# Gates turned by block transposes on VectorE and partition-exchanging DMAs, in a two-layer attention and convolution encoder on one core

## The chip, the cores and the metric

One core of a Trainium2 chip. The metric is the device time of one execution in microseconds (us), the median over runs.

## The reference: what is computed

Two layers (DEPTH 2), a sequence of 512 rows, model width 2048, all fp32. Each layer normalises the rows, multiplies them by one wide input projection, and cuts the result into latents, convolution inputs, memory queries and a gate as wide as the three groups' outputs together:

```python
h = rmsnorm(x, pre_norm_g[l])
z = h @ w_in[l]
q_lat, kv_lat, k_pe, gb, gc, xin, q_mem, gate = split_cols(z)
...
a_out = mla_attention(q, k, v)                 # 8 heads, width 1024
c_out = short_gated_conv(gb, gc, xin, conv_w[l])   # width 512
m_out = memory_attention(q_mem..., mem_n, w_mk[l], w_mv[l])   # 4 heads, width 512
y = jnp.concatenate([a_out, c_out, m_out], axis=-1) * jax.nn.silu(gate)
o = y @ w_o[l]
x = x + rmsnorm(o, post_norm_g[l])
```

The heads' outputs are needed with the features on the partitions (the output projection contracts over them), while the input projection leaves the gate with the sequence's rows on the partitions. So the gate has to be transposed before it multiplies a head's output.

## The kernel before, in words

**Products.** Every fp32 product is made of three matmuls of fp32r parts on TensorE (PE): high by high, low by high, high by low (`mm3`, lines 271 to 273). The large projections are made by a scheme of seven products P1 to P7 over 2x2 blocks. The input projection of a layer is five groups of columns, `gs[0]` to `gs[4]`, each two slabs of 512 columns wide (the fourth 416). `gs[2]` makes the memory heads' gate `gm` and the memory queries `qm`; `gs[4]`, in the code `g4`, makes the attention heads' gates `ga0` and `ga1` in 28 steps. A product ends with a function `final(i, j, tt)` for each finished tile of 128 rows; for these two groups it did nothing (`skip`).

**Order of the work.** A program of steps is written out in Python. `put` adds steps in a row, `weave` adds extra steps among others, `add` adds one. Each step names the weights (units) that it reads. A weight is loaded by SP's queue (line 145) some units ahead of its use, cast to its high part by ScalarE (ACT, line 188, `wh`) and its low part by VectorE (DVE, line 189, `wl`) two units ahead. Some weights are sums, and their second term is added by an accumulating DMA from GpSimd's queue (line 145 too, POOL). A step may put small work into a deferring queue (`pr.defer`), which is emptied as later steps leave room, or until a condition holds (`pr.until`). PE, SP and POOL run in the order in which the program wrote their instructions; ACT and DVE are put in order by a scheduler.

**The gate.** The result of a group stands in slabs of 128 partitions x 2048 (19 buffers), four row tiles of 512 columns. `gate_turn` (line 897) makes one quarter of a gate slab: `turn4` (line 886) transposes four tiles of 128x128 on PE into one bank of PSUM (line 889), and ACT takes Silu of the bank into the slab `y` (line 900). A slab thus takes 16 transposes and four Silus, a layer has three slabs. The memory heads' (`gm`) is turned at the end of the input projection; those of `ga0` and `ga1` in `mixer` (line 1214): `ga0` between the two rope products, `ga1` behind the second.

**The start of the mixer.** `mixer` first makes the rotated part of the queries for four heads: two products (`qr`), whose sums with the rope tables are made on DVE (lines 1019 to 1029) and split into `qrh` on ACT and the rest `rm` on DVE (lines 276 and 277). Then come the four memory heads, among whose steps the first pair of attention heads is prepared (`qkv`: two products for Q, two for K, two for V). A head has four query blocks. Each block is a score product (`sc`), its row maximum on DVE (line 1134, `nm`), exp with the row sum on ACT (line 1137), a reciprocal on DVE (line 1139, `rec`), a scaling on ACT (line 1140), transposes of the probabilities on PE (line 1150, `ptp`), and their split into high on ACT and low on DVE (lines 276 and 277, `PT`). When a memory head's four blocks are there, PE multiplies them with the values (`o`), and DVE multiplies the result by the gate (line 1165, `y<-o,y`). In the memory heads the blocks are handled in a pipeline: transposes follow their score three blocks later, and the first head's `o` stands behind the ninth score.

## Time and profile before

| | before |
|---|---|
| time, median of 3 runs | 1473.28 us (1473.27 to 1473.75) |
| the profiled execution's span | 1471.1 us; no time beside the span is recorded for it |
| PE busy | 1459.6 us, 99% |
| DVE / ACT / POOL busy | 1087.0 / 863.3 / 269.5 us |
| granted TensorE clock | 0.9 or more of full speed in every slice |
| 16 DMA engines | 288.91 MB in 142655 packets |

The span is that of one profiled execution, from its first to its last instruction; the medians are taken over other runs and count what lies around the span. A row of a timeline gives start, duration, engine, line, operation, what it writes and reads, and in brackets how long the engine sat idle before it and what ended that. Names are the program's with buffer numbers left out.

### The profile page before, as it was taken

The numbers are of one execution on the slowest core, as the hardware profiler recorded it, in microseconds if no ns is written. First come the engines' busy times: TensorE is split into PE (matmuls) and PEld (weight loads), VectorE is DVE, ScalarE is ACT, GpSimd is POOL, SyncE is SP. The second block draws the span as 40 slices with busy tenths as digits, with TensorE's granted clock in tenths as the row PEclk, the third lists the DMA queues.
The fourth block names the chain that finished last, engine by engine and source line by source line (L and its number), as shares of the span: only waits on it lengthen the run. The fifth ranks groups of instructions, "written<-read, shape, count | busy, mean of one in ns | idle before, by whom it ended". The sixth has DMA issues, their size and how long they took to land.

```text
span 1471.1 us, 19497 instructions
## 1 busy us (share of the span) xinstructions
PE 1459.6 (99%) x7200; PEld 1247.5 (85%) x7200; DVE 1087.0 (74%) x1445; ACT 863.3 (59%) x1316; POOL 269.5 (18%) x276
## 2 busy tenths in 40 slices
PE   9999999999999999999999999999999999999997
PEld 8888888899888888888898888888988888888886
DVE  5899677957557778868789666776575577788687
ACT  7856343445459788654777434434364686786443
POOL 0032302032301010321210333030322000003111
PEclk9999999999999999999999999999999999999999
DMA  9999979697964292695987999696979554128945
GB/s 358 402 274 225 218 185 187 171 187 221 207 202 107 79 275 89 124 231 154 339 290 228 232 234 222 194 177 161 206 200 216 171 142 104 40 87 155 262 112 186
DMA packets 142655, 288.91 MB, mean 196 GB/s; under 512 B 9888, under 2 KB 32928, under 8 KB 138720
## 3 DMA queue, kind: packets, MB, share of 16 engines
q0 software_dynamic: 56576, 129.51, 43.9%
q1 hardware_dynamic: 85984, 158.16, 33.0%
q8 instruction: 56, 0.92, 0.2%
q14 instruction: 39, 0.32, 0.1%
HBM read 266.01 MB, written 21.63 MB: 196 GB/s over the span
## 4 chain that ended last, share of the span: by engine, by line
PE 96%; DMA 2%; DVE 1%; ACT 0%; SPq 0%; issue 0%; POOLq 0%; DVEq 0%; ACTq 0%
PE P L271 23%; PE P L272 23%; PE P L273 23%; PE ptp L1150 2%; PE tps L889 2%; PE o L272 1%; PE sc L271 1%; PE sc L272 1%; PE sc L273 1%; PE o L273 1%; PE o L271 1%; PE qps L271 1%; PE sc L1131 1%; PE qps L272 1%; PE qps L273 1%; PE sc L1132 1%
## 5 line engine op out<-in xcount | busy, mean ns | idle before, releaser
L188 ACT CAST wh<-wr 128x1024 fp32r<-128x1024 f32 (+2 forms) x436 | 445.4, 1024 | 458.0 <-PE P L273 363.4
L189 DVE TENSOR_TENSOR wl<-wr,wh 128x1024 fp32r<-128x1024 f32 (+2 forms) x436 | 516.0, 1186 | 261.3 <-ACT wh L188 258.0
L271 PE MATMUL P<-wh,S 128*128 128x512 f32 (+1 forms) x896 | 345.1, 385 | 0.0
L272 PE MATMUL P<-wl,S 128*128 128x512 f32 (+1 forms) x896 | 343.7, 384 | 0.0
L273 PE MATMUL P<-wh,S 128*128 128x512 f32 (+1 forms) x896 | 343.2, 383 | 0.0
L271 PE MATMUL P<-wh,A 128*128 128x512 f32 (+1 forms) x656 | 253.0, 386 | 0.0
L272 PE MATMUL P<-wl,A 128*128 128x512 f32 (+1 forms) x656 | 251.8, 384 | 0.5 <-DVE wl L189 0.5
L273 PE MATMUL P<-wh,A 128*128 128x512 f32 (+1 forms) x656 | 251.7, 384 | 0.0
L145 POOL DMA_DIRECT2D wr<-in_w_in_dram x132 | 158.3, 1200 | 439.6 <-DVE wl L189 324.4
L273 PEld LDWEIGHTS P<-wh,S 128*128 128x128 f32 x896 | 168.2, 188 | 30.5
L272 PEld LDWEIGHTS P<-wl,S 128*128 128x128 f32 x896 | 168.2, 188 | 29.5
L271 PEld LDWEIGHTS P<-wh,S 128*128 128x128 f32 x896 | 168.1, 188 | 29.5
L272 PEld LDWEIGHTS P<-wl,A 128*128 128x128 f32 x656 | 123.2, 188 | 22.9 <-DVE wl L189 1.3
L273 PEld LDWEIGHTS P<-wh,A 128*128 128x128 f32 x656 | 123.1, 188 | 22.4
L271 PEld LDWEIGHTS P<-wh,A 128*128 128x128 f32 x656 | 123.1, 188 | 21.7 <-ACT og L579 0.2
L145 POOL DMA_DIRECT2D wr<-in_w_o_dram x40 | 48.5, 1258 | 297.8 <-DVE wl L189 290.9
L1137 ACT ACTIVATE P<-sc,nm 128x512 f32<-128x512 f32 (+1 forms) x96 | 59.7, 623 | 26.0 <-DVE nm L1134 25.7
L1140 ACT ACTIVATE P<-P,rec 128x512 f32<-128x512 f32 (+1 forms) x96 | 62.0, 659 | 8.3 <-DVE rec L1139 8.0
L1134 DVE TENSOR_REDUCE nm<-sc 128x1 f32<-128x512 f32 (+1 forms) x96 | 56.9, 593 | 12.5 <-PE sc L1132 9.6
L1150 PE MATMUL ptp<-identr,P 128*128 128x128 f32 x320 | 46.1, 272 | 0.0
L177 DVE TENSOR_TENSOR wr<-wr,wr 128x1024 f32<-128x1024 f32 (+1 forms) x36 | 42.3, 1177 | 4.5 <-DMA wr<-in_w_in_dram 3.9
L1150 PEld LDWEIGHTS ptp<-identr,P 128*128 128x128 f32 x320 | 38.0, 140 | 6.1
(318 smaller groups left out, 2072.3 us busy)
## 6 DMA issues: line engine op xcount, KB each, us to landing
wr<-in_w_in_dram SPq DMA_DIRECT2D x128, 512.0 KB, 5.4
wr<-in_w_in_dram POOLq DMA_DIRECT2D x108, 512.0 KB, 7.3
wr<-in_w_o_dram SPq DMA_DIRECT2D x48, 512.0 KB, 6.6
wr<-in_w_o_dram POOLq DMA_DIRECT2D x40, 512.0 KB, 6.9
wr<-in_w_in_dram SPq DMA_DIRECT2D x32, 416.0 KB, 3.7
wr<-in_w_in_dram POOLq DMA_DIRECT2D x24, 416.0 KB, 6.0
wr<-in_w_mk_dram SPq DMA_DIRECT2D x15, 512.0 KB, 8.6
wr<-in_w_mv_dram SPq DMA_DIRECT2D x15, 512.0 KB, 10.2
```

Of the source, the lines that this page charges most:

```text
L145: engine.dma_start(dst, src, **kw)
L177: nc.vector.tensor_tensor(tiles[a], tiles[a], tiles[b], op=ALU.add)
L188: pin(nc.scalar.copy(hi[:, h], src[:, h]))
L189: pin(nc.vector.tensor_tensor(lo[:, h], src[:, h], hi[:, h].bitcast(F32), op=ALU.subtract))
L271: nc.tensor.matmul(ps, ah, bh, start=first, stop=False, **kw)
L272: nc.tensor.matmul(ps, ah, bl, start=False, stop=False, **kw)
L273: nc.tensor.matmul(ps, al, bh, start=False, stop=last, **kw)
L889: nc.tensor.transpose(ps[:, t * P:(t + 1) * P], view(t)[:, j * P:(j + 1) * P], G["ident"])
L1134: nc.vector.tensor_reduce(nmax, ps, axis=AX.X, op=ALU.max, negate=True)
L1137: nc.scalar.activation(pt, ps, AF.Exp, bias=nmax, accum_out=tot)
L1140: nc.scalar.activation(pt, pt, AF.Copy, scale=rec)
L1150: nc.tensor.transpose(ps[:, k * P:(k + 1) * P], pt[:, k * P:(k + 1) * P], G["ident"])
```

## The change

The gates' slabs are stored in another order of columns (`p (c t k)`, viewed as four row tiles of 4x128). When a product of `gs[2]` or `gs[4]` ends, `gated` applies Silu on ACT, in place, or for the last products of `ga0` directly from PSUM (which leaves out a copy), and defers one DVE instruction that transposes the 32x32 blocks of the tile in place (`blocks_turned`, line 920 of the changed file). When all four tiles of a slab are so turned, `exchange` (line 922) sends 16 DMAs on SP's queue, one for each pair of a group of 32 partitions as source and one as destination; each moves 32 partitions x 16 runs x 32 elements, that is 64 KB in pieces of 128 bytes. They write the slab `y` that `gate_turn` wrote before. Three slabs per layer make 96 DMAs in all, 24 block transposes, and 96 transposes fewer on PE. The exchange of `gm` stands in the program behind step 13 of `g4`, that of `ga1` behind the first product for Q, that of `ga0` behind the fourth block of the memory heads. Without gates to turn, `mixer` puts the two rope products and their sums one behind the other, and the first product for Q ahead of the first score.

```diff
@@ input projection
         def own(*names):
             def f():
                 for n in names:
-                    C[n] = slab(n).rearrange("p (t c) -> p t c", t=NT)
+                    C[n] = slab(n).rearrange("p (c t k) -> p t c k", c=4, t=NT)
             return f
...
+        def gated(*names):
+            def fin(i, j, tt, ps=None):
+                if names[j] is None:
+                    return
+                v = C[names[j]][:, 2 * i + tt]
+                nc.scalar.activation(v, v if ps is None else ps, AF.Silu)
+
+                def turn():
+                    blocks_turned(v)
+                    C[names[j], "turned"] = C.get((names[j], "turned"), 0) + 1
+                pr.defer(0.7, turn)
+            return fin
+
+        fin_m, fin_a = gated("gm", None), gated("ga0", "ga1")
...
-            group(L, (l, 2), 512, block((O_G + 1536, O_QM), 512), slot_of("gm", "qm"), STEADY, skip),
+            group(L, (l, 2), 512, block((O_G + 1536, O_QM), 512), slot_of("gm", "qm"), STEADY, fin_m),
...
-            group(L, (l, 4), 512, block((O_G, O_G + 512), 512), slot_of("ga0", "ga1"), STEADY, skip),
+            group(L, (l, 4), 512, block((O_G, O_G + 512), 512), slot_of("ga0", "ga1"), STEADY, fin_a, direct=direct_a),
...
-    def gate_turn(j, view, c):
+    def blocks_turned(v):
+
+        nc.vector.transpose(v, v)
+
+    def exchange(dst, src):
+
+
+        for p in range(4):
+            for b in range(4):
+                a = src[32 * p:32 * p + 32].rearrange("i t c k -> i (c t) k")[:, :, 32 * b:32 * b + 32]
+                y = dst[32 * b:32 * b + 32].rearrange("i c (t k) -> i (c t) k", k=P)[:, :, 32 * p:32 * p + 32]
+                nc.sync.dma_start(y, a)
+
+    def gate_rows(k, name, C):
         def f():
-            ps = turn4(view, c)
-            nc.scalar.activation(y_slab(j // 4)[:, j % 4, :], ps, AF.Silu)
+            pr.until(lambda: C.get((name, "turned")) == NT)
+            exchange(y_slab(k), C[name])
         return f
...
@@ mixer
-    def mixer(l, C, gates, pair2, tail):
+    def mixer(l, C, pair2, tail):
...
-        gs = [(g, []) for g in gates]
         (p0, rotate0, fetch0), (p1, rotate1, fetch1) = (q_rope_steps(l, g) for g in range(2))
-        put(p0[:1], gs[:4], p0[1:])
-        put(rotate0, gs[4:])
+        put(p0, rotate0)
         sts = [{} for _ in range(4)]
         qkv = qkv_steps(l, 0, sts[0])
         qkv[0] += (0.0, 1)
         qkv[2] += (0.0, 0)
+        put(qkv[:1])
+        add(gate_rows(1, "ga1", C))
...
-        between = {k: [s] for k, s in zip((0, 2, 5, 8, 10, 12), qkv)}
+        between = {k: [s] for k, s in zip((2, 5, 8, 10, 12), qkv[1:])}
+        between.setdefault(3, []).append((gate_rows(0, "ga0", C), []))
...
-        put(g4[8:16])
+        put(g4[8:13])
+        add(gate_rows(3, "gm", C))
+        put(g4[13:16])
...
-        more = [(f, []) for f in lat + [qm_turn(j, C) for j in range(4)] + [gate_turn(12 + j, gm, j) for j in range(4)]]
-        put(weave(g4[16:], more[:12], 2, 2))
-        put(more[12:])
-        gates = [gate_turn(j, lambda t, C=C, j=j: C["ga0" if j < 4 else "ga1"][:, t, :], j % 4) for j in range(8)]
+        more = [(f, []) for f in lat + [qm_turn(j, C) for j in range(4)]]
+        put(weave(g4[16:], more, 2, 2))
```

In `group`, the PSUM bank is viewed as 4x128 where the slot is; `turn4` and the convolution read the new views.

**How it moves instructions.** Lines from 1103 on are 34 higher in the changed file: its exp is L1171, its scaling L1174, its row maximum L1168. First ACT at the start of layer 0's memory heads, from the table load to the first casts of transposed probabilities (`PT`). Before (`P<-sc,nm` is an exp, `P<-P,rec` a scaling):

```order
L1137 ACT_TABLE_LOAD
L1137 ACTIVATE P_3811,tot_3812<-sc_3805,nm_3809 128x256
L276 CAST Q_3819<-qps_3820 128x512
L1140 ACTIVATE P_3811<-P_3811,rec_3814 128x256
L1137 ACTIVATE P_3841,tot_3842<-sc_3835,nm_3839 128x256
L1137 ACTIVATE P_3853,tot_3854<-sc_3847,nm_3851 128x256
L1140 ACTIVATE P_3841<-P_3841,rec_3844 128x256
L1140 ACTIVATE P_3853<-P_3853,rec_3856 128x256
L276 CAST Q_3819<-qps_3859 128x512
L276 CAST PT_3886<-ptp_3887 128x2x128
L1137 ACTIVATE P_3880,tot_3881<-sc_3874,nm_3878 128x256
L276 CAST PT_3886<-ptp_3904 128x2x128
```

The changed kernel, from the first exps to the first casts; the rows left out are three more exps, seven scalings and the second cast for Q:

```order
L1171 ACT_TABLE_LOAD
L1171 ACTIVATE P_3810,tot_3811<-sc_3804,nm_3808 128x256
L1171 ACTIVATE P_3822,tot_3823<-sc_3816,nm_3820 128x256
L1174 ACTIVATE P_3810<-P_3810,rec_3813 128x256
...
L1171 ACTIVATE P_3913,tot_3914<-sc_3907,nm_3911 128x256
L1171 ACTIVATE P_3943,tot_3944<-sc_3937,nm_3941 128x256
L1171 ACTIVATE P_3965,tot_3966<-sc_3959,nm_3963 128x256
...
L1171 ACTIVATE P_3983,tot_3984<-sc_3977,nm_3981 128x256
L1174 ACTIVATE P_3983<-P_3983,rec_3986 128x256
L276 CAST PT_3884<-ptp_3885 128x2x128
L276 CAST PT_3884<-ptp_3902 128x2x128
L276 CAST K_3922<-kps_3923 128x512
```

The first PT cast stood behind three exps and three scalings; it now stands behind nine of each.

Second, DVE at the same place, around the first row maximum (`nm`); `rm` is the rope sum, `wl` a weight's low part. Before:

```order
L1024 TENSOR_TENSOR qr_3755<-qr_3755,tab_3705 128x512
L1029 TENSOR_TENSOR rm_3768<-rm_3768,qr_3717 128x512
L1028 TENSOR_TENSOR rm_3768<-rm_3768,qr_3755 128x512
L1134 TENSOR_REDUCE nm_3809<-sc_3805 128x1
L189 TENSOR_TENSOR wl_4151<-wr_3538,wh_4150 128x1024
L277 TENSOR_TENSOR rm_3768<-rm_3768,qrh_3774 128x1024
L1134 TENSOR_REDUCE nm_3839<-sc_3835 128x1
L1139 RECIPROCAL rec_3814<-tot_3812 128x1
```

The changed kernel:

```order
L1063 TENSOR_TENSOR rm_3757<-rm_3757,qr_3731 128x512
L1062 TENSOR_TENSOR rm_3757<-rm_3757,qr_3744 128x512
L189 TENSOR_TENSOR wl_4149<-wr_3571,wh_4148 128x1024
L277 TENSOR_TENSOR Q_3771<-qps_3772,Q_3771 128x512
L277 TENSOR_TENSOR rm_3757<-rm_3757,qrh_3763 128x1024
L1168 TENSOR_REDUCE nm_3808<-sc_3804 128x1
L1168 TENSOR_REDUCE nm_3820<-sc_3816 128x1
L1168 TENSOR_REDUCE nm_3832<-sc_3828 128x1
L1168 TENSOR_REDUCE nm_3859<-sc_3855 128x1
L1173 RECIPROCAL rec_3813<-tot_3811 128x1
```

The first row maximum followed the two rope sums; now a weight's low part, the first half of Q and the rope remainder stand ahead of it. Four row maxima stand ahead of the first reciprocal (`rec`), where there had been two.

Third, SP's queue in layer 0, from the last loads of the input projection to the mixer's first weights. Before:

```order
L145 DMA wr_3240<-in_w_in_dram 128x2x512
L145 DMA wr_3277<-in_w_in_dram 128x2x512
L145 DMA wr_3468<-in_w_qr_dram 128x1024
L145 DMA wr_3486<-in_w_uq_dram 128x4x128 x2
...
L145 DMA wr_3601<-in_w_qr_dram 128x1024
L145 DMA wr_3633<-in_w_uq_dram 128x4x128 x2
L145 DMA wr_3652<-in_w_ukv_dram 128x2x512
L145 DMA wr_3711<-in_memt_dram 128x512
L145 DMA wr_3817<-in_memt_dram 128x512
L145 DMA wr_3921<-in_w_uq_dram 128x4x128 x2
```

The changed kernel:

```order
L145 DMA wr_3248<-in_w_in_dram 128x2x512
L145 DMA wr_3285<-in_w_in_dram 128x2x512
L929 DMA y_3327<-gm_1830 32x16x32 x16
L145 DMA wr_3501<-in_w_qr_dram 128x1024
L145 DMA wr_3519<-in_w_uq_dram 128x4x128 x2
...
L145 DMA wr_3638<-in_w_qr_dram 128x1024
L145 DMA wr_3670<-in_w_uq_dram 128x4x128 x2
...
L145 DMA wr_3725<-in_memt_dram 128x512
L145 DMA wr_3769<-in_memt_dram 128x512
L929 DMA y_3787<-ga_124_3022 32x16x32 x16
L929 DMA y_3867<-ga_123_3021 32x16x32 x16
L145 DMA wr_3919<-in_w_uq_dram 128x4x128 x2
```

The exchange of `gm` stands between the last load for the input projection and the first for the mixer; those of `ga1` and `ga0` stand behind two memory tiles and ahead of the second weight for Q.

More of the change, by code (lines that the diff above doesn't have):

```diff
@@ L542, in ended @@
             s = {(i, j): slot(i, j, tt) for i in range(2) for j in range(2)}
+            if len(s[0, 0].shape) == 3:
+                ps = ps.rearrange("p (c k) -> p c k", c=4)
             if q == "P1":
@@ L744, in f @@
                 for n in names:
-                    C[n] = slab(n).rearrange("p (t c) -> p t c", t=NT)
+                    C[n] = slab(n).rearrange("p (c t k) -> p t c k", c=4, t=NT)
             return f
         def slot_of(a, b):
-            return lambda i, j, tt: C[(a, b)[j]][:, 2 * i + tt, :]
+            return lambda i, j, tt: C[(a, b)[j]][:, 2 * i + tt]
         def fin_u(i, j, tt):
@@ L755, in fin_u @@
             if C[key] == 2:
-                nc.vector.tensor_tensor(C["gc"][:, t, :], C["gc"][:, t, :], C["xi"][:, t, :], op=ALU.mult)
+                nc.vector.tensor_tensor(C["gc"][:, t], C["gc"][:, t], C["xi"][:, t], op=ALU.mult)
         def fin_g(i, j, tt):
@@ L762, in fin_g @@
             if j == 1:
-                nc.scalar.activation(C["gg"][:, t, :], C["gg"][:, t, :], AF.Silu)
+                nc.scalar.activation(C["gg"][:, t], C["gg"][:, t], AF.Silu)
             if C[key] == 2:
-                nc.vector.tensor_tensor(C["gb"][:, t, :], C["gb"][:, t, :], C["gg"][:, t, :], op=ALU.mult)
+                nc.vector.tensor_tensor(C["gb"][:, t], C["gb"][:, t], C["gg"][:, t], op=ALU.mult)
         def own_lat():
@@ L772, in projection, with direct_a @@
         skip = lambda i, j, tt: None
+        def gated(*names):
[10 more added lines that the diff above has]
+        fin_m, fin_a = gated("gm", None), gated("ga0", "ga1")
+        def direct_a(i, j, tt, ps):
+            fin_a(i, j, tt, ps)
         L = G["left"]
@@ L888, in turn4 @@
         for t in range(NT):
-            nc.tensor.transpose(ps[:, t * P:(t + 1) * P], view(t)[:, j * P:(j + 1) * P], G["ident"])
+            v = view(t)
+            nc.tensor.transpose(ps[:, t * P:(t + 1) * P], v[:, j] if len(v.shape) == 3 else v[:, j * P:(j + 1) * P], G["ident"])
         return ps
@@ L904, in f @@
         def f():
-            u = turn4(lambda t: C["gc"][:, t, :], c)
+            u = turn4(lambda t: C["gc"][:, t], c)
             y, w = y_slab(2)[:, c, :], G[f"cw{l}"]
@@ L910, in f @@
                                            op0=ALU.mult, op1=ALU.add)
-            g = turn4(lambda t: C["gb"][:, t, :], c)
+            g = turn4(lambda t: C["gb"][:, t], c)
             nc.vector.tensor_tensor(y, y, g, op=ALU.mult)
@@ L918, in f @@
                 G["Qm"] = tuple(slab(n, F32R).rearrange("p (i c) -> p i c", i=4) for n in ("QmH", "QmL"))
-            ps = turn4(lambda t: C["qm"][:, t, :], j)
+            ps = turn4(lambda t: C["qm"][:, t], j)
             hi, lo = G["Qm"][0][:, j, :], G["Qm"][1][:, j, :]
@@ L1538, in encoder @@
         add(lambda C=C: k_rope(C))
-        put(g4[8:16])
+        put(g4[8:13])
+        add(gate_rows(3, "gm", C))
+        put(g4[13:16])
         lat = [latent_turn(l, "cq", j) for j in range(4)] + [latent_turn(l, "ckv", j) for j in range(2)] + [k_rope_turn]
-        gm = lambda t, C=C: C["gm"][:, t, :]
-        more = [(f, []) for f in lat + [qm_turn(j, C) for j in range(4)] + [gate_turn(12 + j, gm, j) for j in range(4)]]
-        put(weave(g4[16:], more[:12], 2, 2))
-        put(more[12:])
-        gates = [gate_turn(j, lambda t, C=C, j=j: C["ga0" if j < 4 else "ga1"][:, t, :], j % 4) for j in range(8)]
+        more = [(f, []) for f in lat + [qm_turn(j, C) for j in range(4)]]
+        put(weave(g4[16:], more, 2, 2))
         G["left"] = Y = Left(False)
@@ L1567, in encoder @@
             add(lambda: G.update(mTd=dram.tile([4, P, D], F32, name="mTd")))
-        mixer(l, C, gates, {3: [(use_y, []), (low(0), [])], 7: [(low(1), [])]}, last_pair)
+        mixer(l, C, {3: [(use_y, []), (low(0), [])], 7: [(low(1), [])]}, last_pair)
         add(sums(1))
```

## The prediction

> **What bounds the kernel now.** I read the page first: busy times, then the chain that ended last.
>
> ```profile
> span 1471.1 us, 19497 instructions
> PE 1459.6 (99%) x7200; PEld 1247.5 (85%) x7200; DVE 1087.0 (74%) x1445; ACT 863.3 (59%) x1316; POOL 269.5 (18%) x276
> PE 96%; DMA 2%; DVE 1%; ACT 0%; SPq 0%; issue 0%; POOLq 0%; DVEq 0%; ACTq 0%
> ```
>
> TensorE (PE) is busy 99% of the span and is 96% of the chain. So an instruction taken from PE shortens the kernel by its own duration, as long as what PE does next is ready that much earlier. That condition is the whole question here, because PE has no other idle time that could take up a delay. The second view is the chain of waits, cut to the mixer's start in layer 0 (rows at 430 us) and in layer 1 (1160 us): start, duration, what.
>
> ```profile
> 432.19 2.19 PE tps L889 x20
> 437.14 1.75 PE tps L889 x16
> 441.66 1.75 PE tps L889 x16
> ...
> 1161.54 2.18 PE tps L889 x20
> 1166.49 1.75 PE tps L889 x16
> 1171.01 1.75 PE tps L889 x16
> ```
>
> Line 889 is the transpose on PE. Sixteen of them turn one slab of the gate; the rows of 20 hold four of the memory queries as well, which stay. The chain passes through all three groups in both layers.
>
> **Removed from PE.** 16 transposes take 1.75 us, 0.109 each (20 take 2.19). Three groups per layer make 3 x 1.75 = 5.25 us, and two layers 10.5 us. That is all there is to gain: 1471.1 - 10.5 = 1460.6 us of span.
>
> **What PE meets next.** After the removed groups come the memory heads: scores, softmax, transposes of the probabilities, and then the first product with the values, `o`. That product needs the four casts of head 0's transposed probabilities (PT) on ScalarE (ACT). The timelines of ACT, VectorE (DVE) and PE from the end of the second rope product to that `o`, in layer 0:
>
> ```profile
> 441.70 0.70 DVE L1023 TENSOR_TENSOR qr<-qr,tab 128x512 f32<-128x512 f32 x1 [2.92 <-PE qr L273]
> 444.10 0.41 DVE L1134 TENSOR_REDUCE nm<-sc 128x1 f32<-128x256 f32 x1
> 444.43 1.21 DVE L189 TENSOR_TENSOR wl<-wr,wh 128x1024 fp32r<-128x1024 f32 x1
> 445.56 1.22 DVE L277 TENSOR_TENSOR rm<-rm,qrh 128x1024 fp32r<-128x1024 f32 x1
> 447.79 0.69 DVE L277 TENSOR_TENSOR Q<-qps,Q 128x512 fp32r<-128x512 f32 x1
> ...
> 446.72 0.47 ACT L1137 ACTIVATE P<-sc,nm 128x256 f32<-128x256 f32 x1
> 448.06 0.47 ACT L1137 ACTIVATE P<-sc,nm 128x256 f32<-128x256 f32 x1
> 448.51 0.48 ACT L1137 ACTIVATE P<-sc,nm 128x256 f32<-128x256 f32 x1
> 448.96 0.91 ACT L1140 ACTIVATE P<-P,rec 128x256 f32<-128x256 f32 x2
> 450.00 0.59 ACT L276 CAST Q<-qps 128x512 fp32r<-128x512 f32 x1
> 454.24 0.65 ACT L276 CAST PT<-ptp 128x256 fp32r<-128x256 f32 x2
> ...
> 456.08 0.48 PE L271 MATMUL o<-PT,Vm 128*128 128x512 f32 x1
> ```
>
> Before, the ACT order between the first exp (446.72) and the last of the four PT casts (454.24 + 0.65 = 454.89) holds 6 exps, 5 scalings (L1140), 2 Q casts, one K cast and the 4 PT casts: 8.17 us. The last cast's remainder on DVE ends about 0.5 us after it, at 455.4, and PE comes to `o` at 456.08, so ACT leads by only 0.7 us. The scheduler that orders ACT gives the changed kernel another order there: 9 exps and 9 scalings, one Q cast, one K cast, then the 4 PT casts. Three exps more (448.51 - 448.06 = 0.45 each, 1.35), four scalings more (0.91 for two less their overlap, about 0.41 each, 1.64), one Q cast less (about 0.5): 8.17 + 2.5 = 10.7 us.
>
> And it starts not 5.25 us earlier but less. Only two of the three groups stand ahead of the second rope product, so that ends 3.5 us earlier, at 438.2, and the five DVE steps on it (2.4 us, 441.70 to 444.10) end at 440.6. The first row maximum (L1134) came directly behind them; now a weight's remainder (pitch 445.56 - 444.43 = 1.13), Q's remainder (0.6) and the rope remainder (1.15) stand ahead of it: 440.6 + 2.9 = 443.5. The first exp goes at about 443.95 instead of 446.72, 2.8 earlier.
>
> So the last PT cast ends at 443.95 + 10.7 = 454.6, its remainder 0.5 later, and `o` can start at about 455.1. PE would be there at 456.08 - 5.25 = 450.8, so it waits 4.3 us. What remains is 5.25 - 4.3, about 1.0 us per layer. That is the upper end; ACT's 8.17 us also held short waits that are kept, and one grows: in the new DVE order four row maxima stand ahead of the first reciprocal, and the fourth needs a score that PE makes after Q's second product (12 matmuls behind the third score), so the first scaling waits some 0.6 us more than it did. That leaves 0.3 to 1.0 per layer; I take 0.5, and 1.0 us for both. Behind `o` nothing gives the rest back, since PE is packed from there (25.00 of 25 us in the window from 444, quoted below).
>
> **Added to DVE.** 24 block transposes of 128x512 in place. The trace has none; the nearest row is the product with the gate, a 128x512 tensor read and written in SBUF:
>
> ```profile
> L1165 DVE TENSOR_TENSOR y<-o,y x24: 669/687/692, 457.8 to 1332.2; 128x512 f32<-128x512 f32 x24
> L900 ACT ACTIVATE y<-tps x24: 587/602/642, 433.2 to 1173.2; 128x512 f32<-128x512 f32 x24
> 265.00:285.00 20.00, 20.00 (x90) 16.55 (x89) 19.34 (x53) 8.82 (x10) 0.00 (x0) 1.00 0.61 175
> 376.00:402.00 26.00, 26.00 (x120) 21.61 (x120) 12.87 (x12) 12.08 (x14) 10.74 (x9) 1.00 1.05 201
> 400.00:432.00 32.00, 32.00 (x165) 26.89 (x164) 21.42 (x25) 17.55 (x24) 2.89 (x4) 1.00 0.71 189
> 444.00:469.00 25.00, 25.00 (x157) 22.23 (x156) 19.27 (x55) 23.66 (x70) 3.67 (x6) 1.00 0.57 127
> ```
>
> I take 0.69 us, with half and twice that as bounds (0.34 and 1.4). 24 x 0.69 = 16.5 us of DVE. The window rows give PE, weight loads, DVE, ACT and POOL busy. The last gate's eight transposes per layer (5.5 us, 11 at the upper bound) fall at 400 to 432, where DVE has 32 - 21.4 = 10.6 us free; at the upper bound weights come late there and I allow up to 5 us. The memory gate's four fall at 265 to 285, where DVE is full (19.3 of 20). They stand among the rope tables, which are wanted much later; cost 0 at 0.69. Uncovered, they would cost 2.8 us.
>
> [...]
>
> **Moved on ACT.** 24 Silus (L900, 0.60 each) move from the mixer's start into the in-projection, where ACT is at 17.6 of 32 and 12.1 of 26 us. Cost 0: they hide in that idle time. Four copies out of PSUM go.
>
> **Added to the queues.** Each slab is exchanged by 16 DMAs on SP's queue, each of 512 pieces of 128 bytes: 8192 pieces, 512 for each of 16 engines. No transfer of the trace has that form. Its neighbours are w_uq loaded alone (pieces of 512 bytes) and a 32-partition load of 2 KB pieces, and the accumulating loads that the exchange meets; the rows are packets, MB and busy share in windows of 0.8, 7.7 and 26 us:
>
> ```profile
> q1 hardware_dynamic: 370, 0.19, 85.4%
> q0 software_dynamic: 576, 1.05, 84.7%
> q0 software_dynamic: 2165, 4.17, 94.6%
> ...
> 350.32 28.17 SPq L145 DMA_DIRECT2D wr<-in_w_in_dram  x8
> 402.60 0.34 SPq L145 DMA_DIRECT2D wr<-in_w_qr_dram  x1
> 406.22 0.92 SPq L145 DMA_DIRECT2D wr<-in_w_uq_dram  x2
> wr<-in_w_uq_dram SPq DMA_DIRECT2D x16, 256.0 KB, 3.4
> 500.14 0.68 DVE L1165 TENSOR_TENSOR y<-o,y 128x512 f32<-128x512 f32 x1
> ```
>
> 0.854 x 0.8 us x 16 / 370 = 29.5 ns for 512 bytes; 0.847 x 7.7 x 16 / 576 = 181 ns for 2 KB, a sixteenth of which is 11 ns. By bytes 128 are 7.4 to 11 ns; if the piece and not its bytes is what costs, 30 ns, and up to 50 if writing to 32 partitions costs more again (the 2 KB row pays 1.5 times the bytes' price). Per slab 3.8, 5.8, 15 or 26 us. I take 5.8: it is the row that also goes into 32 partitions. On SP 16 issues at 0.46 (0.92 for two) are 7.4 us. The memory gate's stand behind the eighth weight load, which leaves at 350.32 + 28.17 = 378.5, and SP is then idle until 402.60: nothing waits. The other two slabs' are followed on SP by w_uq and memory tiles, which are loaded several units ahead of their use; cost 0. The memory gate's slab is first read at 457.8 (L1165), over 70 us later; the other two leave at about 441 to 456 and are read by the attention heads, behind the four memory heads, from 500.14.
>
> What does wait is the train of accumulating loads: the 376 to 402 row has the engines 94.6% busy with it. In layer 1 its last load is the tightest:
>
> ```profile
> 1129.61 1.20 POOL L145 DMA_DIRECT2D wr<-in_w_in_dram  x1 [1.51 <-DVE wl L189]
> wr<-in_w_in_dram POOLq DMA_DIRECT2D x1, 512.0 KB, 9.4
> 1139.56 1.05 ACT L188 CAST wh<-wr 128x1024 fp32r<-128x1024 f32 x1 [1.59 <-PE P L273]
> 1145.69 0.39 PE L271 MATMUL P<-wh,S 128*128 128x512 f32 x1
> ```
>
> It lands at 1139.0, is cast at 1139.56, and PE uses it at 1145.69; cast and remainder take 2.3 of the 6.1 us between, so it may come 0.5 + 3.8 = 4.3 us late. An exchange of 5.8 us, less what the engines had free (5.4% of some 24 us, 1.3), makes it 4.5 late: cost 0.2 per layer at most, and less where the transfers overlap. I count 0.
>
> [...]
>
> **Sum.** 10.5 removed, 2 x 4.75 given back at the first `o`, 0 from DVE, ACT and the queues: 1.0 us. The span of 1471.1 lies 2.2 under the median 1473.28, in which the start and end outside the span are counted; 1473.3 - 1.0 = 1472.3 us.
>
> **The rivals.**
>
> (a) Slower: the exchange delays the accumulating loads and PE waits for a weight at the end of the in-projection. It decides from 4.3 us of delay. At 25 ns a piece the exchange takes 12.8 us, the load is 12.8 - 1.3 - 4.3 = 7.2 late for each layer if it bears the whole, half that if the two share: 1472.3 + 7 = 1479, up to 1487; at 30 ns 1484. For it: the 94.6%; the 512-byte piece costs 29.5 ns, and if that is the floor of a piece, this is the case. Against it: by bytes it is 7 to 11 ns. Chance 0.22. A second way to be slower is that the 16 transfers of a slab land one after another, each as long as w_uq's load (3.4 us): 54 us a slab. That hides for the memory gate (378 + 54 = 432, before 457.8), but the other two would be there at 441 + 109 = 550 instead of 500, some 50 us lost per layer, 1573. Against it: two w_uq loads leave 0.46 us apart and both are there in 3.4, so transfers of a queue overlap. Chance 0.02.
>
> (b) Faster: ACT keeps ahead of `o` and PE doesn't wait, 1473.3 - 10.5 = 1462.8; or it waits half as long, if the maximum isn't as late as I put it and the waits within the 8.17 us vanish, 1473.3 - 2 x (5.25 - 2.6) = 1468. For it: the gates' Silus no longer stand on ACT ahead of the first exp. Against: the order, in which the casts stand behind nine exps, and ACT at 23.66 of 25 us from 444 on. 0.14, nearly all for half.
>
> (c) All is given back: the first `o` comes when it came before, or the exchange takes the last microsecond, 1473.3. It lies in my forecast's own range, 1471 to 1475.
>
> **How the numbers follow.** The forecast with (c) has 0.62, (a) 0.24, (b) 0.14. No change means within 0.2%, 2.9 us, about what a measurement of this kernel can tell. Faster by more (under 1470.3) 0.14; slower by more (over 1476.2) 0.24. The range leaves out 1462.8 and 1573, and goes from 1469.0 (a little of (b)) to 1482 (most of (a) up to 27 ns a piece). The forecast's own range is 1471 to 1475.
>
> **What would show it.** PE has some 96 instructions less and no L889 at the gate; at the first `o` of each layer it waits about 4 us for the PT remainder, with ACT running nine exps and scalings without a break. If (a) holds, PE waits for a weight (L189) near 416 and 1146 and the accumulating loads land in over 12 us instead of 7 to 9. The 24 transposes show their own row near 0.69 us. I am wrong if PE runs into `o` without a wait, if the exchange's pieces take over 25 ns each, or if waits appear at a place not named here.

## The result, and the profile after

The changed kernel takes 1476.2 us (median of 13 runs, 1475.07 to 1477.81), the kernel before 1473.32 (13 runs, 1472.57 to 1474.64): a ratio of 1.0019, 95% interval 1.0011 to 1.0028. It is slower by about 2.9 us; 1.0 us faster was forecast, with a range of 1469.0 to 1482.0. The profile page of the changed kernel, span, busy times and chain:

```profile
span 1473.8 us, 19452 instructions
PE 1454.6 (99%) x7104; PEld 1239.6 (84%) x7104; DVE 1102.1 (75%) x1469; ACT 862.1 (58%) x1312; POOL 269.9 (18%) x276
PE 95%; DMA 2%; DVE 1%; ACT 1%; issue 0%; SPq 0%; POOLq 0%; DVEq 0%; ACTq 0%
```

PE lost its 96 transposes (7200 to 7104 instructions) but only 5.0 us of busy time, and the span grew by 2.7. The view of waits, PE alone (line waited for, total, times, longest):

```profile
PE o L271 <- ACT PT L276: 3.7, 2, 1.9
PE ptp L1184 <- ACT P L1174: 2.3, 2, 1.1
...
PE P L272 <- DVE wl L189: 1.4, 3, 0.7
PE o L272 <- DVE PT L277: 0.7, 2, 0.3
```

Before, PE waited in no mixer. Now it stands at the first `o` of each layer (the first product of the memory heads with the values) and at the first transposes of the probabilities (`ptp`), 6.7 us in all. That alone would leave 10.5 - 6.7 = 3.8 us of gain. Where the rest went is seen by setting the starts of the same instructions side by side. Timelines of PE and DVE before: the convolution's first transposes, the latents', the memory queries', and the gate product of an attention head, then the same for layer 1 from the latents on:

```profile
223.60 0.60 PE L889 MATMUL tps<-identr,gc 128*128 128x128 f32 x4
400.07 1.03 PE L889 MATMUL tps<-identr,lat 128*128 128x128 f32 x8
425.67 1.03 PE L889 MATMUL tps<-identr,qm 128*128 128x128 f32 x8
545.24 0.67 DVE L1165 TENSOR_TENSOR y<-o,y 128x512 f32<-128x512 f32 x1
1142.08 1.03 PE L889 MATMUL tps<-identr,lat 128*128 128x128 f32 x8
1155.01 1.04 PE L889 MATMUL tps<-identr,qm 128*128 128x128 f32 x8
1287.42 0.67 DVE L1165 TENSOR_TENSOR y<-o,y 128x512 f32<-128x512 f32 x1
```

And of the changed kernel:

```profile
224.01 0.60 PE L910 MATMUL tps<-identr,gc 128*128 128x128 f32 x4
401.43 1.03 PE L910 MATMUL tps<-identr,lat 128*128 128x128 f32 x8
427.04 1.04 PE L910 MATMUL tps<-identr,qm 128*128 128x128 f32 x8
546.45 0.67 DVE L1199 TENSOR_TENSOR y<-o,y 128x512 f32<-128x512 f32 x1
1143.17 1.04 PE L910 MATMUL tps<-identr,lat 128*128 128x128 f32 x8
1156.10 1.04 PE L910 MATMUL tps<-identr,qm 128*128 128x128 f32 x8
1289.76 0.67 DVE L1199 TENSOR_TENSOR y<-o,y 128x512 f32<-128x512 f32 x1
```

| stretch | before | changed | difference |
|---|---|---|---|
| start to 1st row | 223.60 | 224.01 | +0.41 |
| rest of the in-projection, layer 0 (1st to 2nd row) | 176.47 | 177.42 | +0.95 |
| mixer, layer 0 (3rd to 4th row) | 119.57 | 119.41 | -0.16 |
| mixer, layer 1 (6th to 7th row) | 132.41 | 133.66 | +1.25 |

The first 0.4 us stands ahead of anything that the change touches; in the other kernels of this study the same stretch differs from the first kernel's by -1.3 to +2.1, so it is scatter. The other three are the subject: +0.95, -0.16 and +1.25. The two mixers wait alike, yet differ by 1.4 us. The windows around the wait give the reason (the window, its length, then busy PE, weight loads, DVE, ACT and POOL; the number behind them is the granted clock, as a share of full speed). The first row is layer 0, the others layer 1:

```profile
455.00:460.00 5.00, 3.12 (x18) 2.59 (x19) 4.53 (x11) 2.99 (x10) 0.00 (x0) 1.00 1.58 140
1185.00:1190.00 5.00, 4.06 (x14) 3.34 (x15) 3.70 (x9) 1.80 (x6) 0.00 (x0) 0.68 1.41 150
1190.00:1195.00 5.00, 5.00 (x41) 4.92 (x41) 3.30 (x11) 4.51 (x16) 0.00 (x0) 0.98 0.72 105
```

Behind the wait at `o` in layer 1 the clock of PE fell to half (0.51 in the window from 1186.82 to 1190.23, shown further down) for 2 x (0.32 + 0.02) x 5 = 3.4 us; at half speed that would lose 1.7 us, and the two mixers differ by 1.4. In layer 0 the same wait had no such sequel (1.00).

### The profile page after: what moved, and what is told of

The parts are those of the page before. It is cut to its first block, busy times and chain, and to the rows that moved or that the text cites. A ratio compares the mean times of both kernels' runs of the same rounds, so it can differ in the third digit from the quotient of the medians.

```text
span 1473.8 us, 19452 instructions
## 1 busy us (share of the span) xinstructions
PE 1454.6 (99%) x7104; PEld 1239.6 (84%) x7104; DVE 1102.1 (75%) x1469; ACT 862.1 (58%) x1312; POOL 269.9 (18%) x276
## 4 chain that ended last, share of the span: by engine, by line
PE 95%; DMA 2%; DVE 1%; ACT 1%; issue 0%; SPq 0%; POOLq 0%; DVEq 0%; ACTq 0%
PE P L272 23%; PE P L273 23%; PE P L271 23%; PE ptp L1184 2%; PE o L272 1%; PE o L273 1%; PE sc L273 1%; PE sc L271 1%; PE sc L272 1%; PE o L271 1%; PE tps L910 1%; PE sc L1165 1%; PE qps L272 1%; PE qps L271 1%; PE qps L273 1%; PE sc L1166 1%
## 5 line engine op out<-in xcount | busy, mean ns | idle before, releaser
L1171 ACT ACTIVATE P<-sc,nm 128x512 f32<-128x512 f32 (+1 forms) x96 | 59.2, 617 | 30.3 <-DVE nm L1168 29.7
L1168 DVE TENSOR_REDUCE nm<-sc 128x1 f32<-128x512 f32 (+1 forms) x96 | 56.9, 596 | 13.3 <-PE sc L273 7.1
L1174 ACT ACTIVATE P<-P,rec 128x512 f32<-128x512 f32 (+1 forms) x96 | 60.6, 652 | 6.6 <-DVE rec L1173 6.6
## 6 DMA issues: line engine op xcount, KB each, us to landing
wr<-in_w_mv_dram SPq DMA_DIRECT2D x15, 512.0 KB, 10.5
```

Source lines behind the costliest of these rows:

```text
L1168: nc.vector.tensor_reduce(nmax, ps, axis=AX.X, op=ALU.max, negate=True)
L1171: nc.scalar.activation(pt, ps, AF.Exp, bias=nmax, accum_out=tot)
L1174: nc.scalar.activation(pt, pt, AF.Copy, scale=rec)
```

## The experiments

Each kernel was timed against the kernel before on the same chip, whose median there was 1473.3 to 1473.7 us. Theory A at the outset: the gain is given back at the first `o` by ACT's order. Rival B: the exchanges' transfers cost the time. Kernels e2, e3, e6 and e10 leave out part of the gate's transposition; they serve for their times alone.

**e1: ga0's exchange later.**

```diff
-        between.setdefault(3, []).append((gate_rows(0, "ga0", C), []))
+        between.setdefault(9, []).append((gate_rows(0, "ga0", C), []))
```

> The exchange of ga0 moves from behind the fourth block of the memory heads to behind the tenth; nothing else changes. In the order of ScalarE, 7 exps and 6 scalings then stand ahead of the fourth cast of transposed probabilities, where the changed kernel has 9 and 9. Theory A (the gain is given back at the first product with the values, by ScalarE's order, and the half clock in layer 1 follows from that stall): the wait falls by 2 x 0.45 + 3 x 0.41 = 2.1 us per layer, and the half clock's 1.6 us go: 1476.2 - 4.2 - 1.6 = 1470.4 us. Rival B (the exchanges' transfers and SP's late weights cost the time): they are all still there, 1476 or more.

Measured 1477.89 us, ratio 1.0035 (1.0023 to 1.0047): slower than the changed kernel, where 1470.4 had been expected. PE's longest wait:

```profile
PE sc L271 <- DVE V L277: 5.4, 2, 2.7
```

The wait at the first `o` is gone, as expected, but a larger one stands at the first attention head's score, for V's cast: ACT's order puts it behind three more exps, three scalings and two weight casts, just behind the new place of the exchange. Both mixers had a half clock (from 470.6 and from 1201.1, 3.4 us each). So the order of ACT is where the wait is, but what disturbs that order moves along with the exchange.

**e2: one plain DMA per slab.**

```diff
-        for p in range(4):
-            for b in range(4):
-                ...
-                nc.sync.dma_start(y, a)
+        nc.sync.dma_start(dst.rearrange("p j c -> p (j c)"), src.rearrange("p t c k -> p c t k").rearrange("p c t k -> p (c t k)"))
```

> The 16 DMAs of each exchange are replaced by one DMA that copies the slab partition by partition, so the gate is left untransposed across partitions; the place in the program is that of the changed kernel. ScalarE's order comes out as in the kernel with ga0 late. Theory A: the same time as that kernel, 1470.4, within 1 us, because the small pieces cost nothing on the path. Rival B: the pieces and the full queue are gone, 1466 or less, at least 3 us under the kernel with ga0 late.

Measured 1467.42 us, ratio 0.9962 (0.9950 to 0.9974). The gate stays untransposed across partitions. At the same place in the program, with the same 3 MB moved per layer, it is 8.8 us faster than the changed kernel. PE's only wait in the mixers is the first transposes'; the clock stayed full:

```profile
PE ptp L1180 <- ACT P L1170: 2.3, 2, 1.1
```

The mixers take 3.1 us less than before each (427.50 to 543.93, 116.43 us, in layer 0). It is neither theory's number (1470.4, or under 1466), but the sum goes with B: the 16 small DMAs are what costs, through ACT's order or otherwise. The two aren't separated here, because the order changed too: between the first exp and the fourth PT cast ACT has 7 exps and 6 scalings, as in e1, where the changed kernel has 9 and 9.

**e3: no block transposes** (`blocks_turned(v)` taken out, so the gate's blocks stay unturned).

> The 24 block transposes on VectorE are left out, so the gate's blocks stay unturned; ScalarE's order is that of the changed kernel. Theory A: only the wait for a weight's low part near 292 us in layer 0 goes (0.7 to 0.95 us): 1475.3; the stall at the first product with the values stays at about 3.3 us per layer. Rival C (the transposes hold up VectorE where the mixer starts, and so the softmax): 3 us or more faster, 1473 or less, with the stall at that product smaller.

Measured 1475.34 us, ratio 1.0013 (1.0004 to 1.0021), as theory A had it. From the convolution's first transposes to the latents' it takes 176.47 us, as before: the 0.95 us there went with the memory gate's four transposes. The waits at `o` and `ptp` are unchanged (3.7 and 2.3). C falls. This time the half clock came in layer 0, and the two mixers changed places with it: against the kernel before +1.16 us in layer 0 (426.42 to 547.15) and -0.12 in layer 1 (1158.24 to 1290.53).

**e4: ga0 late and the memory gate's transposes held back** until the last group.

```diff
-                pr.defer(0.7, turn)
+                if names[j] == "gm":
+                    C.setdefault("held", []).append(turn)
+                else:
+                    pr.defer(0.7, turn)
...
+        add(lambda C=C: [pr.defer(0.7, turn) for turn in C["held"]] and None)
```

> ga0's exchange late as above, and the four transposes of the memory gate held back until the last group of the input projection, behind the rope tables. Theory A: the time of the kernel with ga0 late less 0.7 to 0.95 us, 1469.5, with no wait for a weight near 292 us. If that wait has another cause, the time stays at 1470.4 and the wait is still there.

Measured 1477.87 us, ratio 1.0030 (1.0019 to 1.0041). The stretch up to the latents is 176.47 us again, so the 0.9 us went; the median doesn't show it, because V's wait of e1 is still there and the half clocks come in one or in both mixers. But in the profiles of e5 and e9, which have the transposes where the change has them, it is 176.47 as well, while e1, e2, e6 and e10, which have them there too, show 176.9 to 177.6. So these transposes cost up to about 1 us in five of seven profiles, and not in every execution.

**e5: ga0's exchange behind the memory heads** (`between.setdefault(16, ...)`).

> ga0's exchange moves behind the last block of the memory heads; all 96 DMAs and 24 block transposes stay. In ScalarE's order the casts of the memory heads then stand as in the kernel with one plain DMA per slab. Theory A, amended (a cast into a new slab that the program writes behind ga0's exchange is put late in ScalarE's order, and PE then waits for it wherever that is; the transfers cost nothing): each layer's mixer gains as much through the memory heads as with the plain DMA, 3.2 us, less about 1 to 1.5 us where the first attention heads meet the same effect; with the 0.9 us of the memory gate's transposes 1473.3 - 6.5 + 0.9 + 2.5 = 1470.2 us, between 1469 and 1472. Rival B (the transfers and the full SP queue cost the time): 1476 or more, and no gain through the memory heads.

Measured 1470.49 us, ratio 0.9979 (0.9970 to 0.9987), as the amended theory had it, with all 96 exchanges and 24 transposes. PE's waits in the mixers:

```profile
PE ptp L1184 <- ACT P L1174: 2.3, 2, 1.1
PE o L272 <- DVE PTl L277: 1.9, 2, 1.2
```

No half clock. The wait at the first `o` is gone, and with it most of what was lost; at the attention heads PE now waits 1.9 us in all, where e2 has no wait. So what the same DMAs cost goes by their place in the program.

**e6: only the memory gate exchanged**, the other two slabs by plain DMAs.

```diff
-            exchange(y_slab(k), C[name])
+            if name == "gm":
+                exchange(y_slab(k), C[name])
+            else:
+                nc.sync.dma_start(y_slab(k).rearrange("p j c -> p (j c)"), C[name].rearrange("p t c k -> p (c t k)"))
```

> The memory gate is exchanged by its 16 DMAs as in the changed kernel, the other two slabs by one plain DMA each (their gates stay untransposed across partitions). ScalarE's order is that of the kernel with plain DMAs alone. Theory A: the same time as that kernel, 1467.4, within 1 us: the 16 small transfers run beside the accumulating loads and PE waits for no weight. Rival B, as it stood in the prediction (the exchange delays the last accumulating loads): 2 us or more slower than that, with PE waiting for a weight near 415 or 1145 us.

Measured 1468.56 us, ratio 0.9958 (0.9944 to 0.9972); e2's interval covers it. The exchange that runs beside the accumulating loads costs nothing that these runs can tell. What costs is that of ga0 and ga1, where the change has them.

**e7: three places changed**: ga0's exchange at 16, the memory gate's transposes held back as in e4, and the first product for Q behind the first score:

```diff
-        put(qkv[:1])
         add(gate_rows(1, "ga1", C))
...
-        between = {k: [s] for k, s in zip((2, 5, 8, 10, 12), qkv[1:])}
+        between = {k: [s] for k, s in zip((0, 2, 5, 8, 10, 12), qkv)}
```

> Three places change: ga0's exchange behind the memory heads, the memory gate's transposes held back to the last group of the input projection, and the first product for Q back behind the first score, so that the first row maximum and the first scaling come earlier. Theory A: no wait near 292 us (0.9 us less than with ga0's exchange moved alone), and the wait at the first transposes of the probabilities falls from 1.1 to about 0.6 us per layer, 1 us in all, and less at the attention heads: 1466 us, between 1465 and 1468. If the waits of ScalarE's order are not what costs, it stays at 1470 or above.

Measured 1466.37 us, ratio 0.9946 (0.9934 to 0.9959): faster than both kernels, by 7.3 and 9.8 us. The three changes aren't separated. PE waits 0.7 us at the first transposes of each layer, and once 1.2 at an attention head:

```profile
PE ptp L1187 <- ACT P L1177: 1.5, 2, 0.7
...
PE o L272 <- DVE PTl L277: 1.2, 1, 1.2
```

**e8: a wait put into the kernel before.**

```diff
+    def stall(n):
+        a = bank("warm")
+        nc.tensor.matmul(a, G["onesr"][:, :P], G["onesr"], start=True, stop=True)
+        s = scrap("st")
+        nc.scalar.copy(s, a)
+        for k in range(n):
+            nc.scalar.copy(s, s)
+        b = bank("warm")
+        nc.tensor.transpose(b[:, :P], s[:, :P], G["ident"])
...
         put(gs[2][0])
+        add(lambda l=l: stall((0, 3)[l]))
```

> The kernel before, with a chain put in behind the first product of the memory gate's group: one matmul, a copy of its result on ScalarE, in layer 1 three more copies in place, and one transpose on PE that needs the last. PE so waits once in each layer, for about 1 us in layer 0 and about 3.8 us in layer 1, and does one matmul and one transpose more. Theory D (a wait of PE of 2.5 us or more is followed by 3.4 us at half clock, which costs another 1.7): half clock once, in layer 1, behind the wait: 1473.3 + 0.7 + 1.1 + 3.8 + 1.7 = 1480.6 us. Rival (the half clock comes from something else in the mixer): no half clock there, 1478.9.

Measured 1481.44 us, ratio 1.0049 (1.0035 to 1.0062). The two waits in PE's timeline, and the windows at the second:

```profile
218.80 0.33 PE L1396 MATMUL warm<-identr,st 128*128 128x128 f32 x1 [0.94 <-ACT st L1392]
953.48 0.48 PE L1396 MATMUL warm<-identr,st 128*128 128x128 f32 x1 [3.70 <-ACT st L1394]
```

```profile
950.00:955.00 5.00, 1.52 (x4) 1.27 (x5) 1.54 (x2) 3.36 (x6) 1.22 (x1) 0.72 1.00 284
955.00:960.00 5.00, 5.00 (x15) 3.92 (x14) 0.00 (x0) 0.89 (x1) 0.00 (x0) 0.59 0.70 116
```

Far from the mixer and its DMAs, the wait of 3.7 us is followed by 2 x (0.28 + 0.41) x 5 = 6.9 us at half clock, the wait of 0.9 us by none. Theory D holds for a wait of this length, with twice the half clock expected; its limit of 2.5 us was the author's estimate, and no run shows it. Between 0.9 and 3.7 us no wait outside the mixer was tried.

**e9: ACT's order held, everything else as changed.** Each exp and scaling of the memory heads from the fifth block on is queued behind the cast of four blocks earlier:

```diff
-                nc.scalar.activation(pt, ps, AF.Exp, bias=nmax, accum_out=tot)
...
+                casts = G.setdefault("casts", [])
+                with tc.issue_after(casts[-1].ins) if rope is None and j > 12 or rope is None and t > 3 else nullcontext():
+                    nc.scalar.activation(pt, ps, AF.Exp, bias=nmax, accum_out=tot)
...
+                    nc.scalar.activation(pt, pt, AF.Copy, scale=rec)
...
-                split_to(hi, lo, ps.rearrange("p (k c) -> p k c", k=kts))
+                src = ps.rearrange("p (k c) -> p k c", k=kts)
+                G.setdefault("casts", []).append(nc.scalar.copy(hi, src))
+                nc.vector.tensor_tensor(lo, src, hi.bitcast(F32), op=ALU.subtract)
```

> The changed kernel with all its DMAs, transposes and places; added is only an order on ScalarE: in the memory heads each exp and scaling from the fifth block on is queued behind the cast of the transposed probabilities of four blocks earlier (order alone, no wait for it to finish). Theory A, amended: the wait at the first product with the values goes, what is left is the first transposes' 1.1 us and some 0.7 us more per layer, and the half clock of layer 1 goes with the stall: a gain of 2.7 us per layer through the memory heads, less 0.9 for the memory gate's transposes, 1473.5 - 5.4 + 0.9 = 1469 us, between 1468 and 1470.5. Rival B (the place of ga0's transfers, not ScalarE's order, delays the casts): the casts then wait for them, and the time stays at 1475 or more.

Measured 1480.03 us, ratio 1.0038 (1.0025 to 1.0052): worse, where 1469 was expected, and on the side of rival B, which had the casts wait for ga0's transfers at 1475 or more. The longest waits of PE, and the V cast in ACT's timeline of layer 0:

```profile
PE ptp L1186 <- ACT P L1176: 8.7, 6, 2.8
```

```profile
462.91 0.58 ACT L276 CAST V<-vps 128x512 fp32r<-128x512 f32 x1 [3.61 <-DMA y<-ga]
```

The wait for PT at the first `o` is gone, so it did come from ACT's order. But with PT and V early, V's cast stood 3.6 us waiting for the exchange, and all that ACT had behind it waited too. In layer 1 it stood 3.4 us. It waited for the exchange of `ga1`: the last of those 16 DMAs landed at 462.66, 0.25 us before V's cast began, while ga0's ran on to 474. In the built program V's tile has the buffer that `ga1` had, which is free only when the exchange has read it. This is a second way in which the same transfers cost, and the amended theory had left it out. Half clock followed in both layers, 6.8 us from 463.4 and 3.4 us from 1197.3.

**e10: the memory gate's exchange sent twice** (e6 with `exchange` called twice).

> As the kernel with the memory gate alone exchanged by small DMAs, but its exchange is sent twice (the second writes the same values again). Theory E (each DMA of SP's queue waits for the one eight places ahead of it to land, so an exchange holds SP's queue for 27 to 31 us, and what it costs is decided by the loads behind it): 32 DMAs hold the queue until about 437 to 442 us, the first weight for the rope product leaves then instead of at 409, and PE waits for it 10 to 17 us in each layer: 1490 to 1505 us with some half clock behind the waits. Rival (SP's queue has room, only the engines' share counts): the accumulating loads come a few us later still, 1470 to 1475.

Measured 1478.93 us, ratio 1.0031 (1.0020 to 1.0043), under the 1490 expected but over the rival's 1475. SP's queue, and the waits of PE that e6 had not:

```profile
378.18 43.55 SPq L929 DMA_DIRECT2D y<-gm  x32
421.83 0.55 SPq L145 DMA_DIRECT2D wr<-in_w_qr_dram  x1
```

```profile
PE qr L271 <- ACT wh L188: 3.3, 2, 1.7
...
PE qr L273 <- DVE wl L189: 1.1, 2, 0.5
```

The queue was held for 43.6 us instead of 27, the first rope weight left at 421.8, and PE waited for it. So a held queue costs, as theory E had it. Its price was too high, since the second 16 DMAs went out in 15 us after 28 for the first 16. And its reason was wrong: in the changed kernel's trace 84 of the 96 DMAs do wait on a counter that the one eight places ahead of them raises, but in e10's that one had landed at least 1.2 us before the issue began. The time is in the issues themselves, 0.63 us each at the end of the train and up to 3.5 us beside the accumulating loads. The memory heads lost time as well: the first transposes waited 5.8 us in all instead of 2.3, and the clock fell to half three times, from 435.1, 452.2 and 1169.0, for 3.4 us each.

## Why the prediction was wrong

**Removed from PE: right.** 96 instructions went. No run measures their 10.5 us alone; the nearest is layer 1 of e7, whose mixer takes 128.01 us (1151.16 to 1279.17) against 132.41, 4.40 less, with one wait of 0.7 us in it: 5.1 together, against 5.25 in the forecast.

**What PE meets next: right in size, in place only in part.** The first exp was put 2.8 us earlier; it starts at 445.40, on a clock that runs 1.37 late there (427.04 against 425.67), which is 2.7 earlier than 446.72. `o` was put at 455.1; it starts at 456.54 - 1.37 = 455.17, and its second matmul waits 0.34 more for DVE's half (`PT`'s remainder):

```profile
445.40 0.48 ACT L1171 ACTIVATE P<-sc,nm 128x256 f32<-128x256 f32 x1 [0.33 <-DVE nm L1168]
...
456.54 0.50 PE L271 MATMUL o<-PT,Vm 128*128 128x512 f32 x1 [1.86 <-ACT PT L276]
457.38 0.50 PE L272 MATMUL o<-PT,Vm 128*128 128x512 f32 x1 [0.34 <-DVE PT L277]
```

That `o` came within 0.1 us is in part luck. The fourth PT cast ended at 456.48 - 1.37 = 455.11, 0.5 later than forecast, and the first matmul of `o` didn't wait for the remainder, for which 0.5 had been added. Nor was the wait one of 4.3 us at `o`: 1.13 us of it stood at the first transposes (`ptp`), a place that the prediction hadn't named, and 1.86 and 0.34 at `o`. Each wait also breaks the overlap of matmuls that start 0.23 us apart and last 0.39: by start to start, the three cost 1.29, 2.03 and 0.61 us, 3.9 in all. Stops of under 0.25 us each between 451 and 454 add about 0.7. Layer 0's mixer kept 0.16 us of 5.25, where 0.5 was forecast (0.3 to 1.0); some 0.5 of the 5.09 is assigned to nothing.

**The step that failed, first: "Behind `o` nothing gives the rest back".** The prediction priced a wait of PE at its own length and had no term for the clock. Behind the wait in layer 1 came 3.4 us of half clock, 1.4 us by the two mixers' difference. e8 shows that a wait does this by itself.

Why one layer and not the other can be read off the trace's records of the clock. The half-clock stretches begin on a grid of 3.413 us, the length of the changed kernel's one, that runs on from the clock's first rise: in the changed kernel 346 such windows lie between the rise at 5.76 and the fall at 1186.77, and 82 between the rise at 1190.18 and the last fall at 1470.08; in the kernel before 428 between the rise at 6.28 and the only fall, at 1467.18; in e8 277. The starts given above lie 214 windows apart in e1, 215 in e9, 5 and 210 in e10. Here are windows of that grid, the one with most of the wait in layer 0, then the same in layer 1 and the one behind it (length, busy PE, and the clock behind POOL's column):

```profile
452.93:456.34 3.41, 1.74 (x8) 0.95 (x6) 1.47 (x6) 3.18 (x11) 0.00 (x0) 1.00 1.67 194
1183.40:1186.81 3.41, 1.20 (x5) 0.61 (x6) 2.57 (x8) 3.11 (x9) 0.00 (x0) 0.99 1.63 202
1186.82:1190.23 3.41, 3.41 (x14) 3.04 (x13) 1.93 (x5) 0.45 (x2) 0.00 (x0) 0.51 1.24 122
```

In layer 0 a border of the grid cuts the wait in two, and PE is idle for 1.7 us of the first window; in layer 1 the wait lies in one window, with 2.2 us idle, and the next one runs at half clock. Over all profiles but their first and last microseconds, each of the nine windows with 2.1 us idle or more was followed by half clock, two of five with 1.6 to 1.9, and at full clock none with less. By these windows the length of a wait doesn't decide alone, but where it falls on the grid, and for one of this length that is luck.

The profiled run was a mild one. Each run has a mean granted clock: 0.998 or 0.999 in all 44 runs of the kernel before that were taken beside the experiments, 0.998 in the profiled run of the changed kernel, but 0.996 in eight of its 13 runs. A stretch of 3.4 us at half clock lowers the mean by 1.7 / 1474 = 0.0012, so most runs had about two of them, an estimate from rounded figures.

**The step that failed, second: "cost 0" on DVE. The price was right, the cover wasn't.** Rows of the changed kernel's lines:

```profile
L920 DVE STREAM_TRANSPOSE ga<-ga x16: 670/705/716, 386.3 to 1163.3; 128x512 f32<-128x512 f32 x16
L920 DVE STREAM_TRANSPOSE gm<-gm x8: 696/704/706, 244.2 to 1021.0; 128x512 f32<-128x512 f32 x8
```

0.70 us against 0.69 forecast. But "cost 0" for the memory gate's four, on a VectorE with 19.3 of 20 us busy, was wrong in this profile: 0.95 us, gone in e3 and e4, though also absent in e5 and e9, where the transposes stand. The prediction had the uncovered price beside it (2.8 us) and didn't use it. (The 0.109 us that it took for a transpose on PE is the distance from start to start in a train of them; each lasts 0.27 us in the same trace.)

**Added to the queues: the price was wrong, the cost in this kernel was right.** "16 issues at 0.46 (0.92 for two) are 7.4 us. [...] nothing waits." In the changed kernel:

```profile
379.90 30.98 SPq L929 DMA_DIRECT2D y<-gm  x16
411.00 1.83 SPq L145 DMA_DIRECT2D wr<-in_w_qr_dram  x1
443.56 28.61 SPq L929 DMA_DIRECT2D y<-ga  x32
472.35 1.04 SPq L145 DMA_DIRECT2D wr<-in_w_uq_dram  x2
```

The memory gate's issues took 30.98 / 16 = 1.94 us each, ga's 0.89 (0.63 us each at the end of the train). From issue to landing a DMA of 64 KB took 8.8 us beside the accumulating loads and 3.1 us for ga's, which met none of them (medians; in layer 0 nine such loads left between 376 and 411 us and none between 440 and 473):

```profile
y<-ga SPq DMA_DIRECT2D x64, 64.0 KB, 3.1
y<-gm SPq DMA_DIRECT2D x32, 64.0 KB, 8.8
```

So an exchange holds the queue for 14 to 31 us where 7.4 was put down. What sets the pace of the issues stays open: it isn't the counters, since for each of the changed kernel's 96 the DMA eight places ahead had landed 0.2 us or more before the issue began.

The memory gate's last one landed 36 us after its first issue, with several under way at once; ga1's 16 were through in 18 us.

A piece of 128 bytes costs 0.589 x 29 us x 16 / 14402 = 19 ns (the row below: queue, packets, share of the window from 441 to 470 us, nearly all of them such pieces), inside the bounds of 7.4 to 50, over the 11 that was taken:

```profile
q1 hardware_dynamic: 14402, 2.04, 58.9%
```

Rival (a), the late accumulating load, came close and didn't decide: ACT stood 4.3 us waiting for one, and PE did not. (Its 1484 us at 30 ns a piece doesn't follow by its own working: 15.4 - 1.3 - 4.3 = 9.8 us, that is 1482 when the two share.)

```profile
415.35 2.00 ACT L188 CAST wh<-wr 128x1024 fp32r<-128x1024 f32 x2 [4.33 <-DMA wr<-in_w_in_dram]
```

In the changed kernel no instruction of PE, ACT or DVE is shown waiting for an exchange; only GpSimd's queue is, 9.0 us in four waits at its accumulating loads. So on PE's path "nothing waits" came true. What the transfers did cost is in ACT's order, which the prediction had read off the built program and counted in its 4.75 us. What it didn't ask is where that order comes from: e2, e5 and e6 show that it comes with the exchanges of ga0 and ga1 at their place, and without them (e2) the mixers gain 3 us each. And e9 shows why the order tried there didn't help: the exchange holds its source, and what takes over the slab's buffer waits until it is read.

**The sum again, for the profiled run:** 10.5 removed; 5.09 + 5.09 given back in the mixers without the clock; 1.4 for the half clock; 0.95 for the transposes: +2.0 us. 0.4 was lost ahead of the change and 0.1 won between the layers, 2.3 us at the last row compared; the rest of the 2.7 lies behind it. Against the 1.0 us of gain that was forecast, 3.0 us are missing in the terms of the sum: 1.4 from the clock, 0.95 from DVE and 0.7 from the two mixers (5.09 for 4.75).

Open is why the scheduler puts the PT casts late when the exchange of ga0 stands where the change has it: the held buffer explains V in e9, but no PT cast of the changed kernel waits for `y<-ga`. Open too is which windows of the unprofiled runs had half clock; the changed kernel's times spread over 2.7 us, those before over 2.1.

## What to carry to other kernels

Price a transfer by how long it holds its source and its queue, not by its bytes: here 16 DMAs of 64 KB held SP's queue for 14 to 31 us, and the buffers they read came free only at the end (V's cast stood 3.6 us for one in e9). Ask who takes those buffers next before finding a place for the transfers; here other places for the same DMAs and transposes and for one product of PE made 9.8 us (e7 against the change). And on a kernel that is bound by PE, look at what follows idle time of PE of about 2 us: here half clock followed each of the nine windows of 3.413 us with 2.1 us idle or more, and two of the five with 1.6 to 1.9.

## What the runs showed of the hardware that was not expected

- A wait of PE of 3.7 us was followed by 6.9 us at half clock (e8); one of 1.9 us with another of 0.3 by 3.4 us in layer 1 and by none in layer 0 (changed kernel), and the other way round in e3; one of 0.9 us by none.
- The half clock came in windows of 3.413 us, one or two behind one another (3.4 us, and 6.8 to 6.9), on the grid counted above, behind each of the nine windows in which PE was idle for 2.1 us or more (2.15 to 2.80).
- 64 KB from 32 partitions to 32 partitions in 128-byte pieces landed in 3.1 us (median) with no accumulating load beside them, and in 8.8 us with them (nine between 376 and 411 us). Issuing one took SP 0.59 us at the least and up to 4.2 us, although the DMA eight places ahead of it had landed 0.2 us or more before.
- A block transpose of 128x512 fp32 on VectorE took 0.70 us in place.
